# A 31-tap depthwise convolution computed as a product of spectra in a one-core transformer kernel

## The chip, the core and the metric

The kernel runs on one core of a Trainium2 chip. A core has TensorE (matrix products, called PE in the profile, with PEld for its weight loads), VectorE (DVE), ScalarE (ACT), GpSimd (POOL) and SyncE (SP, which here only issues DMAs). The metric is the device time of one execution in microseconds (us), from the chip; lower is better.

## The reference, cut to what matters

Two transformer blocks run one after the other over 256 tokens of width 1024. The change touches the odd layer of the second block alone: its mixer, which runs once, near the end of the program.

```python
def odd_mixer(u, conf_dw, conf_dw_b, conf_ln_g, conf_ln_b, sc_dw):   # u = h @ b_w_in, 256 x 2560
    a, gate, sb, scc, sx = jnp.split(u, [512, 1024, 1536, 2048], axis=-1)
    conf = a * jax.nn.sigmoid(gate)
    conf = depthwise_conv(conf, conf_dw) + conf_dw_b        # 31 taps, 512 channels, over tokens
    conf = jax.nn.silu(group_layer_norm(conf, conf_ln_g, conf_ln_b, 4))   # 4 groups of 128 channels
    sc = sb * depthwise_conv(scc * sx, sc_dw)               # 3 taps
    return jnp.concatenate([conf, sc], axis=-1)

x = x + g1 * (odd_mixer(h @ b_w_in, ...) @ b_w_out)
x = x + g2 * swiglu(modulate(rms_norm(x, norm2_g), sh2, sc2), ffn_w1, ffn_w3, ffn_w2)
```

A depthwise convolution mixes nothing between channels: each output token of a channel is a weighted sum of 31 neighbouring tokens of that channel.

## The kernel before, in words

The function `phase_f` holds the odd layer. It opens its pools, normalises the tokens (`rms_affine`: sums of squares on ACT, a chain of small operations and the scaled rows `xr` on DVE, transposes `aT` on PE, then `ut`, `lhs_hi` on ACT and `lhs_lo` on DVE), runs the products with `b_w_in`, the mixer, the product with `b_w_out` (`residual`) and then the feed-forward part (`ffn(1)`), which ends the program.

Every large product is made from three products of fp32r parts: `split` copies a weight tile `w` to `whi` on ACT (L201), subtracts on DVE or POOL to get `wlo` (L202), and PE multiplies whi by lhs_hi, wlo by lhs_hi and whi by lhs_lo. A tile `w` is 1 MB: it is loaded by an SP DMA into a ring of four (`wtile`), and split in two halves of 128x1024; there are three buffers for halves here. Behind each tile of the layer's weights one tile of another weight, `ada_w`, is loaded and multiplied (`pump`, rate 1), a background job for the feed-forward part. Two forms of product appear in the layer:

- `lin_T`: weights stationary, output with channels on the partitions and 256 tokens along the row (lines L1899 to L1901, 128x256, 48 PE instructions for each 1 MB tile).
- `products`, called by `lin` and `lin_D`: tokens stationary, output with tokens on the partitions and 512 channels along the row (lines L246 to L248, 128x512, 24 PE instructions for each 1 MB tile).

The ten tiles of `b_w_in` go through five calls of `lin_T`: two with half of the gate and half of the value each (`ev_conf`), then `scc`, `sx` and `sb` for the three-tap part. All their halves are split on POOL. `ev_conf` sets the gate on ACT (`osg`), multiplies on DVE into `oconf` with 15 columns of zeros on either side, and then convolves channel block by channel block: 29 of 31 taps are DVE instructions over 128x256 (`conv`: L1947 and then L1945 into `ocv`), and `TAPS` = 2 taps are products with diagonal matrices `odw` on PE (L1968 into `oconv`). After the last `lin_T`, PE adds the transposed `ocv` into `oconv` (L1992). `head_norm` is the group norm (L1485 to L1492, into `oct`), PE transposes `oct` into `oT`, ACT applies silu (L2000, into `osl`), and `split_T` makes the parts for `residual`.

The Tile framework sets the order of each engine's instructions from the order of the code and its readiness; each engine then runs its own queue strictly in order. PSUM has four banks for accumulators (`A`) and four for everything else (`B`).

## Time and profile before

| | |
|---|---|
| time, median of 3 runs | 2397.98 us (2395.06 to 2399.15) |
| time of the profiled execution | 2396.94 us, of which the profile's span is 2395.2 us |
| PE busy over the span | 2199.4 us (92%), 13153 instructions |
| DVE busy | 1287.0 us (54%) |
| ACT, POOL busy | 745.4 us (31%), 459.3 us (19%) |
| bytes read from HBM | 646.58 MB, 270 GB/s over the span |
| mean granted TensorE clock | 0.960 of full |
| place of the odd mixer | about 2035 to 2190 us of the span; `ffn(1)` follows to the end |

Times in rows are counted from the start of the span. A row of a group gives a line, an engine, an operation, its output and inputs by the program's names, and the number of instructions behind an x. One product of fp32 numbers that the code writes appears as two PE instructions in the trace; the fp32r products appear as one.

### The profile page before, as it was taken

The page shows a single profiled execution, that of the slowest core. Times are in us where ns is not written, and L with a number is a line of the kernel's source. Part 1 is how long each engine was busy: PE and PEld are TensorE (multiplying, and loading weights), DVE is VectorE, ACT ScalarE, POOL GpSimd, SP SyncE. Part 2 cuts the span into 40 slices and gives each one's busy share as a digit, 9 for nine tenths or more (in the row PEclk, how much of TensorE's full clock was granted, in tenths as well). Part 3 has the DMA queues.
Part 4 walks back from the last instruction along what each step waited for, and adds up shares of the span by engine and source line. Part 5 has one row for each costly group of instructions (what it writes and reads, how often), then busy time and mean ns, then how long its engine had stood idle before and what let it go on. Part 6 is the DMA issues. An engine that isn't in the chain of part 4 may idle for free.

```text
span 2395.2 us, 35469 instructions
## 1 busy us (share of the span) xinstructions
PE 2199.4 (92%) x13153; PEld 1383.5 (58%) x13154; DVE 1287.0 (54%) x3006; ACT 745.4 (31%) x1263; POOL 459.3 (19%) x424
## 2 busy tenths in 40 slices
PE   7999996899899997999799899997999999868999
PEld 3686774444444442776543333332756997656997
DVE  3354756655466556757833222225764554766554
ACT  2215233211211111444331111111463443414443
POOL 2121300133233335101001211112101000650000
PEclk9999998899999998999899999998999999979999
DMA  8654267799999998443599999999545555737553
GB/s 297 245 203 170 72 214 271 275 377 408 348 408 409 409 409 333 163 176 124 223 356 408 362 408 408 409 409 349 200 148 194 187 184 188 265 117 250 185 179 120
DMA packets 208891, 650.31 MB, mean 272 GB/s; under 512 B 20796, under 2 KB 34093, under 8 KB 197184
## 3 DMA queue, kind: packets, MB, share of 16 engines
q1 hardware_dynamic: 201680, 632.24, 70.4%
q0 software_dynamic: 7024, 15.66, 1.9%
q8 instruction: 107, 1.75, 0.3%
q14 instruction: 80, 0.66, 0.1%
HBM read 646.58 MB, written 1.25 MB: 270 GB/s over the span
## 4 chain that ended last, share of the span: by engine, by line
PE 49%; DMA 13%; DVE 8%; ACT 1%; POOL 1%; issue 1%; SPq 0%; DVEq 0%; ACTq 0%; POOLq 0%
PE gu L842 10%; DMA w<-in_moe_w_up_dram 8%; PE ey L868 5%; PE A L246 4%; PE A L247 4%; PE A L248 4%; PE A L1901 4%; PE A L1900 4%; PE A L1899 4%; DMA w<-in_moe_w_down_dram 4%; DVE ocv L1945 2%; PE ada L314 1%; PE xT L768 1%; PE sc L888 1%; DVE wlo L202 1%
## 5 line engine op out<-in xcount | busy, mean ns | idle before, releaser
L842 PE MATMUL gu<-w,xT 128*32 128x512 f32 (+1 forms) x2880 | 480.9, 603 | 24.3 <-DVEq L996 8.9
L202 DVE TENSOR_TENSOR wlo<-w,whi 128x1024 fp32r<-128x1024 f32 (+3 forms) x240 | 294.4, 1228 | 309.6 <-ACT whi L201 309.3
L201 ACT ACTIVATE whi<-w 128x1024 fp32r<-128x1024 f32 (+3 forms) x264 | 274.1, 1041 | 506.3 <-PE A L248 275.7
L842 PEld LDWEIGHTS gu<-w,xT 128*32 128x32 f32 (+1 forms) x2880 | 139.9, 121 | 310.4 <-issue 245.9
L1901 PE MATMUL A<-lhs_hi,wlo 128*128 128x256 f32 x864 | 246.8, 286 | 13.6 <-POOL wlo L202 13.1
L246 PE MATMUL A<-whi,lhs_hi 128*128 128x512 f32 (+3 forms) x640 | 249.5, 394 | 7.8 <-ACT whi L201 4.4
L247 PE MATMUL A<-wlo,lhs_hi 128*128 128x512 f32 (+3 forms) x640 | 246.2, 385 | 4.4 <-DVE wlo L202 4.2
L1899 PE MATMUL A<-lhs_hi,whi 128*128 128x256 f32 x864 | 247.8, 287 | 0.7 <-ACT whi L201 0.7
L1900 PE MATMUL A<-lhs_lo,whi 128*128 128x256 f32 x864 | 247.2, 286 | 0.0
L248 PE MATMUL A<-whi,lhs_lo 128*128 128x512 f32 (+3 forms) x640 | 244.7, 383 | 0.1
L868 PE MATMUL ey<-w,hT 128*32 128x512 f32 (+1 forms) x1440 | 226.6, 598 | 9.3 <-ACT hT L855 9.2
L892 DVE TENSOR_TENSOR gy<-sc,g 128x512 f32<-128x512 f32 x188 | 121.3, 685 | 209.0 <-PE sc L889 207.1
L893 POOL TENSOR_TENSOR mx<-mx,gy 128x512 f32<-128x512 f32 x124 | 161.1, 1326 | 356.3 <-DVE gy L892 356.2
L1901 PEld LDWEIGHTS A<-lhs_hi,wlo 128*128 128x128 f32 x864 | 167.9, 195 | 14.1 <-POOL wlo L202 13.3
L1899 PEld LDWEIGHTS A<-lhs_hi,whi 128*128 128x128 f32 x864 | 168.2, 195 | 6.8 <-issue 5.0
L1900 PEld LDWEIGHTS A<-lhs_lo,whi 128*128 128x128 f32 x864 | 167.9, 194 | 0.2 <-DVE lhs_lo L256 0.2
L246 PEld LDWEIGHTS A<-whi,lhs_hi 128*128 128x128 f32 x640 | 122.0, 192 | 58.7 <-issue 17.9
L868 PEld LDWEIGHTS ey<-w,hT 128*32 128x32 f32 (+1 forms) x1440 | 68.0, 121 | 148.6 <-issue 121.2
L893 POOL TENSOR_TENSOR xres<-xres,gy 128x512 f32<-128x512 f32 x58 | 74.0, 1289 | 378.7 <-DVE gy L892 377.9
L247 PEld LDWEIGHTS A<-wlo,lhs_hi 128*128 128x128 f32 x640 | 122.5, 191 | 32.9 <-DVE wlo L202 7.3
L248 PEld LDWEIGHTS A<-whi,lhs_lo 128*128 128x128 f32 x640 | 122.3, 191 | 24.9 <-issue 4.0
L882 DVE SCALAR_TENSOR_TENSOR yl<-ey,wsl,yh 128x512 fp32r<-128x512 f32 x62 | 46.4, 750 | 139.2 <-ACT yh L881 137.9
(591 smaller groups left out, 3312.7 us busy)
## 6 DMA issues: line engine op xcount, KB each, us to landing
w<-in_moe_w_gate_dram SPq DMA_DIRECT2D x248, 512.0 KB, 10.2
w<-in_moe_w_up_dram SPq DMA_DIRECT2D x248, 512.0 KB, 10.1
w<-in_moe_w_down_dram SPq DMA_DIRECT2D x248, 512.0 KB, 10.2
w<-in_ada_w_dram SPq DMA_DIRECT2D x88, 1024.0 KB, 6.4
w<-in_ffn_w_dram SPq DMA_DIRECT2D x64, 1024.0 KB, 5.1
w<-in_ab_w_in_dram SPq DMA_DIRECT2D x13, 1024.0 KB, 8.5
w<-in_c_w_qkv_dram SPq DMA_DIRECT2D x12, 1024.0 KB, 5.2
w<-in_ada_w_dram SPq DMA_DIRECT2D x16, 512.0 KB, 10.3
```

What stands on the lines that cost most here:

```text
L201: self.nc.scalar.activation(hv, w, AF.Copy)
L202: (eng or self.nc.vector).tensor_sub(lv, w, hv.bitcast(F32))
L246: nc.tensor.matmul(o, hi[:, kk, ts], wh[:, k], start=at + k == 0, stop=False)
L247: nc.tensor.matmul(o, hi[:, kk, ts], wl[:, k], start=False, stop=False)
L248: nc.tensor.matmul(o, lo[:, kk, ts], wh[:, k], start=False, stop=at + k == nk - 1)
L842: nc.tensor.matmul(pgu[m][a:b], xT[:, j, a:b], w[:, i, k], start=j == 0, stop=j == 7)
L868: nc.tensor.matmul(py[h][a:b], hT[:, j, a:b], w[:, i, k, h * 512:h * 512 + 512], start=j == 0, stop=j == 3)
L892: V.tensor_mul(gy, ps, M.g2[t // 2][:, h * 512:h * 512 + 512])
L893: eng.tensor_add(o, o, gy)
L1899: nc.tensor.matmul(o, wh[:, k, cs], hi[:, kk], start=kk == 0 and c % 2 == 0, stop=False)
L1900: nc.tensor.matmul(o, wh[:, k, cs], lo[:, kk], start=False, stop=False)
L1901: nc.tensor.matmul(o, wl[:, k, cs], hi[:, kk], start=False, stop=kk == 7 and c % 2 == 1)
```

## The change

The 31-tap convolution is computed as a product of spectra. Over 272 samples, which hold 256 tokens and 16 zeros, the convolution wraps around without touching a result. Its 136 frequencies lie at odd halves, so that each has a cosine and a sine part. Three tables of constants are added as inputs: `dft_w` takes the taps to spectra, `dft_t` the tokens, `dft_b` goes back. The steps are:

- At the start of the layer six DMAs on POOL's queue load the two tap tables, the three tables of constants and the bias; three fp32 PE products (`oH`, 31 rows by 512 channels) make the spectra of the taps, and ACT copies them. All of it stands ahead of `rms_affine`.
- Gate and value come from `lin`, with tokens on the partitions and 512 channels along the row, in the place of two calls of `lin_T`.
- A generator `conv_norm` does the rest in three steps, called from `lin_T` behind every tile through `self.between`: behind the first tile of `scc` six fp32 products of 512 columns (`oX`, tokens to spectra) and seven DVE operations (spectra times spectra, into `oY`); behind the second tile of `scc` six fp32 products back (`oconv`, the bias is one more row of the product) and both group norms; behind the second tile of `sx` the eight transposes and silu. Nothing is done at the other calls.
- The first tap of the three-tap convolution moves from DVE to ACT.

The diff, cut to what matters:

```diff
@@ lin_T, behind each tile of weights
+            if self.between:
+                next(self.between)
@@ phase_f
-            self.rms_affine(self.xres, 1, 0, lhs)
             with self.pool("pf") as p:
-                wrow = p.tile([34, 512], F32, name="wrow")
-                nc.gpsimd.dma_start(wrow[:31], I["b_conf_dw_2"][0])
-                nc.gpsimd.dma_start(wrow[31:], I["b_sc_dw_2"][0])
...
-                        nc.scalar.activation(dw[:, c, k], self.ident, AF.Copy, scale=cw[:, c, k:k + 1])
...
+                nc.gpsimd.dma_start(fw, I["dft_w"])
+                nc.gpsimd.dma_start(ft, I["dft_t"])
+                nc.gpsimd.dma_start(fb, I["dft_b"])
+                Y = [p.tile([m, 512], F32, name=f"oY{i}") for i, m in enumerate((128, 128, 33))]
+                nc.gpsimd.dma_start(Y[2][32:], I["b_conf_dw_b_2"])
...
+                    nc.tensor.matmul(ph[:m], fw[:, o:o + m], wrow, start=True, stop=True)
+                    nc.scalar.activation(h, ph[:m], AF.Copy)
...
+                self.rms_affine(self.xres, 1, 0, lhs)
...
-                        V.tensor_mul(conf[:, c, 15:271], ps, sg[:, c])
-                        conv(cv, conf, c, range(TAPS, 31), 0, self.pcol[:, 53 + c:54 + c])
-                        for t in range(2):
-                            for k in range(TAPS):
-                                at = k + t * 128
-                                nc.tensor.matmul(pv[t][:, c * 128:c * 128 + 128], conf[:, c, at:at + 128],
-                                                 dw[:, c, k], start=c == 0 and k == 0, stop=False)
+                def ev_conf(t, ps):
+                    V.tensor_mul(conf[:, t], ps, sg[t])
+                def conv_norm():
+                    px = [self.psB("oX") for _ in parts]
+                    for x, (o, m) in zip(px, parts):
+                        for k in range(2):
+                            nc.tensor.matmul(x[:m], ft[:, k, o:o + m], conf[:, k], start=k == 0, stop=k == 1)
+                    V.tensor_mul(Y[0], px[0], H[0])
+                    V.tensor_mul(q[1], px[0], H[1])
+                    V.tensor_mul(q[0], px[1], H[1])
+                    V.tensor_mul(Y[1], px[1], H[0])
+                    V.tensor_mul(Y[2][:32], px[2][:32], H[2])
+                    V.tensor_sub(Y[0], Y[0], q[0])
+                    V.tensor_add(Y[1], Y[1], q[1])
+                    yield
+                    for t in range(2):
+                        for i, (_, m) in enumerate(((0, 128), (0, 128), (0, 33))):
+                            nc.tensor.matmul(pv, fb[:m, i, t * 128:t * 128 + 128], Y[i], start=i == 0, stop=i == 2)
+                        self.head_norm(pv, ct[t], True, 1e-6)
+                    yield
+                    yield
...
-                for c2 in range(2):
-                    self.lin_T(W, ((512 + 256 * c2, 256), (256 * c2, 256)), lhs, each(ev_conf(c2)), nc.gpsimd)
+                self.early = 8
+                self.lin(W, 8, 512, 512, lhs, (0, 1), ev_gate)
+                self.lin(W, 8, 0, 512, lhs, (0, 1), ev_conf)
+                self.between = conv_norm()
                 self.lin_T(W, ((1536, 512),), lhs, each(ev_scc), nc.gpsimd)
                 self.lin_T(W, ((2048, 512),), lhs, each(ev_sx), nc.gpsimd)
                 self.lin_T(W, ((1024, 512),), lhs, each(ev_sb), nc.gpsimd)
```

Setting `self.early` to 8 keeps the eight halves of gate and value on POOL. What stands on DVE from the multiplication with the gate on is, before (`oconf` the gated value, `ocv` the running sum of the taps, `oscx` the input of the three-tap part):

```order
L1963 TENSOR_TENSOR oconf<-A,osg 128x256 x2
L1947 TENSOR_SCALAR ocv<-oconf,cw,pcol 128x256 x2
L1945 SCALAR_TENSOR_TENSOR ocv<-oconf,cw,ocv 128x256 x56
L1963 TENSOR_TENSOR oconf<-A,osg 128x256 x2
L1947 TENSOR_SCALAR ocv<-oconf,cw,pcol 128x256 x2
L1945 SCALAR_TENSOR_TENSOR ocv<-oconf,cw,ocv 128x256 x56
L318 TENSOR_TENSOR ada_sb<-ada,ada_sb 128x512
L1976 TENSOR_TENSOR oscx<-A,oscc 128x256 x2
```

All 116 instructions of the taps stand between the two halves of the gate and the three-tap part. The same place in the changed kernel (`oX` the spectra of the tokens in PSUM, `oH` those of the taps, `oY` their product, `oq` a helper):

```order
L1968 TENSOR_TENSOR oconf<-A,osg_18671 128x512
L1968 TENSOR_TENSOR oconf<-A,osg_18672 128x512
L1977 TENSOR_TENSOR oY_18516<-oX,oH_18522 128x512
L1978 TENSOR_TENSOR oq<-oX,oH_18526 128x512
L1979 TENSOR_TENSOR oq<-oX,oH_18526 128x512
L1980 TENSOR_TENSOR oY_18517<-oX,oH_18522 128x512
L1982 TENSOR_TENSOR oY_18516<-oY_18516,oq 128x512
L1981 TENSOR_TENSOR oY_18518<-oX,oH_18530 32x512
L1983 TENSOR_TENSOR oY_18517<-oY_18517,oq 128x512
L1497 BN_STATS hn_st<-oconv 128x6 x4
L1499 BN_AGGR hn_mv<-hn_st 128x2 x4
```

Seven operations stand in the place of the taps, and the group norm has moved ahead of the three-tap part, behind which it stood before. On PE, the second visit of the taps on its queue is, before, in the middle of a tile of `scc`:

```order
L1901 MATMUL A<-lhs_hi,wlo 128x256
L1968 MATMUL oconv<-odw,oconf 128x128 x8
L1899 MATMUL A<-lhs_hi,whi 128x256
L1900 MATMUL A<-lhs_lo,whi 128x256
L1901 MATMUL A<-lhs_hi,wlo 128x256
```

Whatever stands behind `oconv` there waits with it for DVE's `oconf`. In the changed kernel the first spectral work on PE's queue is between the two tiles of `scc`:

```order
L1913 MATMUL A<-lhs_hi,wlo 128x256
L1975 MATMUL oX<-oconf,dftT 128x512 x4
L1975 MATMUL oX<-oconf,dftT 32x512 x2
L326 MATMUL ada<-w,cs_1104 32x512 x4
L1911 MATMUL A<-lhs_hi,whi 128x256
```

A whole tile of `scc` (48 instructions) now stands between the last value product and `oX`, and another between `oX` and the way back. On ACT, where the halves of the weights are copied to `whi`, the end of the mixer reads before (the last `whi` of `sb` are among the first row's seven, the next belong to `b_w_out`):

```order
L201 ACTIVATE whi<-w 128x1024 x7
L255 ACTIVATE lhs_hi<-osv 128x256 x3
L201 ACTIVATE whi<-w 128x1024
L255 ACTIVATE lhs_hi<-osv 128x256
L201 ACTIVATE whi<-w 128x1024 x3
L2000 ACT_TABLE_LOAD
L2000 ACTIVATE osl<-oT,pcol 128x256 x2
```

The silu stands there behind weights of `b_w_out`. In the changed kernel:

```order
L213 ACTIVATE whi<-w 128x1024 x3
L2020 ACTIVATE osv<-oscx,cw 128x256 x2
L1999 ACT_TABLE_LOAD
L1999 ACTIVATE osl<-oT,pcol 128x256 x2
L267 ACTIVATE lhs_hi<-osl 128x256 x2
L1999 ACTIVATE osl<-oT,pcol 128x256 x2
L267 ACTIVATE lhs_hi<-osl 128x256 x2
L2020 ACTIVATE osv<-oscx,cw 128x256 x2
L213 ACTIVATE whi<-w 128x1024 x4
```

The silu and the first tap `osv` now stand ahead of the last two halves of `sb`, which are the first two of the last row's four.

## Rows read from the trace of the kernel before

**Rows 1.** Busy time by stretch: us, then PE, PEld, DVE, ACT, POOL, clock, DMA share, GB/s.

```profile
2052.00:2190.00 138.00, 109.90 (x756) 90.97 (x758) 96.93 (x220) 45.62 (x70) 67.74 (x28) 0.89 0.57 210
...
2117.30:2130.50 13.20, 0.23 (x2) 0.03 (x1) 11.67 (x29) 1.03 (x1) 13.20 (x1) 0.62 0.00 0
2155.40:2164.30 8.90, 8.90 (x52) 6.59 (x51) 7.20 (x32) 3.51 (x6) 1.17 (x3) 1.00 1.05 402
2199.50:2395.20 195.70, 190.34 (x1325) 177.72 (x1324) 98.34 (x99) 83.11 (x98) 3.55 (x2) 0.99 0.48 159
```

**Rows 2.** The chain of work that ended last, in order of time, 2062 to 2136 us.

```profile
2062.05 0.12 PE A L1900
...
2067.75 36.42 DVE ocv L1945 x55
...
2105.28 3.78 PE oconv L1968 x16
2109.06 0.21 PE A L1899
...
2113.27 17.32 POOL wlo L202
```

**Rows 3.** Waits from 2030 to 2195 us: who waited for whom, us in total, times, longest.

```profile
PE A L1901 <- POOL wlo L202: 13.1, 1, 13.1
PE oconv L1968 <- DVE oconf L1963: 13.1, 1, 13.1
...
PE aT L153 <- DVE xr L1648: 6.0, 1, 6.0
...
PE oT L153 <- DVE oct L1492: 1.9, 1, 1.9
```

**Rows 4.** PE in order of time: start, us, line, operation, count.

```profile
1807.57 1.88 PE L1874 MATMUL fA<-fourT,fU 128*128 128x512 f32 x4
...
2155.52 1.95 PE L1992 MATMUL oconv<-ident,ocv 128*128 128x128 f32 x16
...
2158.39 0.50 PE L246 MATMUL A<-whi,lhs_hi 128*128 128x512 f32 x1
```

**Rows 5.** DVE and POOL groups of the layer: duration of one, ns min/median/max.

```profile
L1945 DVE SCALAR_TENSOR_TENSOR ocv<-oconf,cw,ocv x112: 467/471/2619, 2067.7 to 2127.9; 128x256 f32<-128x256 f32 x112
...
L202 POOL TENSOR_TENSOR wlo<-w,whi x20: 2339/2407/19214, 2039.6 to 2145.6; 128x1024 fp32r<-128x1024 f32 x20
```

**Rows 6.** DVE in order of time, start first.

```profile
2034.16 0.69 DVE L1663 TENSOR_TENSOR gy<-A,gres 128x512 f32<-128x512 f32 x1 [1.88 <-PE A L248]
...
2039.41 4.86 DVE L1642 TENSOR_SCALAR rA<-adaT 128x16 f32<-128x16 f32 x1
...
2140.21 0.76 DVE L1976 TENSOR_TENSOR oscx<-A,oscc 128x256 f32<-128x256 f32 x2 [11.24 <-PE A L1901]
...
2158.77 0.68 DVE L1485 BATCH_NORM_STATS2 hn_st<-oconv 128x6 f32<-128x128 f32 x3
...
2169.91 1.36 DVE L1492 TENSOR_SCALAR oct<-oconv,hn_mv,hr_y 128x128 f32<-128x128 f32 x4
```

**Rows 7.** POOL in order of time.

```profile
2039.58 4.65 POOL L202 TENSOR_TENSOR wlo<-w,whi 128x1024 fp32r<-128x1024 f32 x2
...
2054.87 0.55 POOL L1917 DMA_DIRECT2D wrow<-in_b_conf_dw_dram  x1 [8.02 <-PE aT L153]
...
2136.84 4.77 POOL L202 TENSOR_TENSOR wlo<-w,whi 128x1024 fp32r<-128x1024 f32 x2 [1.60 <-ACT whi L201]
```

**Rows 8.** ACT in order of time.

```profile
2079.00 1.07 ACT L201 ACTIVATE whi<-w 128x1024 fp32r<-128x1024 f32 x1 [3.01 <-PE A L1900]
...
2174.12 1.28 ACT L2000 ACT_TABLE_LOAD   x1
2175.41 1.02 ACT L2000 ACTIVATE osl<-oT,pcol 128x256 f32<-128x256 f32 x2
2176.32 0.72 ACT L255 ACTIVATE lhs_hi<-osl 128x256 fp32r<-128x256 f32 x2
```

More of the change, by code (lines that the diff above doesn't have):

```diff
@@ L31 @@
 C0, E0, E1, F0, F1 = 4, 4, 4, 1, 4
-TAPS = 2
 NSPL = 3
@@ L1913, in phase_f @@
             lhs = self.lhs_pair(256)
[L1914 removed]
             with self.pool("pf") as p:
[L1916 to L1919 removed]
+                wrow = p.tile([31, 512], F32, name="wrow")
+                nc.gpsimd.dma_start(wrow, I["b_conf_dw_2"][0])
@@ L1920, in phase_f @@
+                cw = p.tile([128, 4, 3], F32, name="cw")
                 pt = self.psB("cw")
                 for c in range(4):
-                    self.tr(pt[:, c * 34:c * 34 + 34], wrow[:, c * 128:c * 128 + 128])
-                V.tensor_copy(cw.rearrange("p c k -> p (c k)"), pt[:, :136])
-                sg = p.tile([128, 4, 256], F32, name="osg")
-                dw = p.tile([128, 4, TAPS, 128], F32, name="odw")
-                for c in range(4):
-                    for k in range(TAPS):
-                        nc.scalar.activation(dw[:, c, k], self.ident, AF.Copy, scale=cw[:, c, k:k + 1])
@@ L1929, in phase_f @@
-                pv = [self.psB("oconv") for _ in range(2)]
-                conf = p.tile([128, 4, 286], F32, name="oconf")
-                V.memset(conf[:, :, :15], 0.0)
-                V.memset(conf[:, :, 271:], 0.0)
+                    self.tr(pt[:, c * 3:c * 3 + 3], wsc[:, c * 128:c * 128 + 128])
+                V.tensor_copy(cw.rearrange("p c k -> p (c k)"), pt[:, :12])
+                self.rms_affine(self.xres, 1, 0, lhs)
+                sg = [p.tile([128, 512], F32, name=f"osg{t}") for t in range(2)]
@@ L1933, in phase_f @@
+                conf = p.tile([128, 2, 512], F32, name="oconf")
                 scx = p.tile([128, 4, 258], F32, name="oscx")
@@ new lines, in ev_conf @@
+                def ev_conf(t, ps):
[5 more added lines that the diff above has]
+                            nc.tensor.matmul(x[:m], ft[:, k, o:o + m], conf[:, k], start=k == 0, stop=k == 1)
+                    q = [self.sb.tile([128, 512], F32, name="oq", tag="s512") for _ in range(2)]
+                    V.tensor_mul(Y[0], px[0], H[0])
[6 more added lines that the diff above has]
+                    yield
+                    ct = []
+                    for t in range(2):
+                        pv = self.psB("oconv")
+                        for i, (_, m) in enumerate(((0, 128), (0, 128), (0, 33))):
+                            nc.tensor.matmul(pv, fb[:m, i, t * 128:t * 128 + 128], Y[i], start=i == 0, stop=i == 2)
+                        ct.append(p.tile([128, 512], F32, name=f"oct{t}"))
+                        self.head_norm(pv, ct[t], True, 1e-6)
+                    yield
+                    yield
+                    for c in range(4):
+                        po = self.psB("oT")
+                        for t in range(2):
+                            self.tr(po[:, t * 128:t * 128 + 128], ct[t][:, c * 128:c * 128 + 128])
+                        u = self.sb.tile([128, 512], F32, name="osl", tag="s512")
+                        nc.scalar.activation(u[:, :256], po[:, :256], AF.Silu, scale=self.pcol[:, 57 + c:58 + c],
+                                             bias=self.pcol[:, 61 + c:62 + c])
+                        self.split_T(mix[0][:, c], mix[1][:, c], u[:, :256])
+                    yield
+                    yield
+                    yield
@@ L1987, in phase_f @@
                 self.lin_T(W, ((1024, 512),), lhs, each(ev_sb), nc.gpsimd)
-                ct = [p.tile([128, 512], F32, name=f"oct{t}") for t in range(2)]
-                for t in range(2):
-                    for c in range(4):
-                        nc.tensor.matmul(pv[t][:, c * 128:c * 128 + 128], cv[:, c, t * 128:t * 128 + 128],
-                                         self.ident, start=False, stop=c == 3)
-                    self.head_norm(pv[t], ct[t], True, 1e-6)
-                for c in range(4):
-                    po = self.psB("oT")
-                    for t in range(2):
-                        self.tr(po[:, t * 128:t * 128 + 128], ct[t][:, c * 128:c * 128 + 128])
-                    u = self.sb.tile([128, 512], F32, name="osl", tag="s512")
-                    nc.scalar.activation(u[:, :256], po[:, :256], AF.Silu, scale=self.pcol[:, 57 + c:58 + c],
-                                         bias=self.pcol[:, 61 + c:62 + c])
-                    self.split_T(mix[0][:, c], mix[1][:, c], u[:, :256])
+                self.between = None
             self.residual(I["b_w_out_2"][0], 8, mix, 1, 0)
@@ L2019, in build @@
         self.first = None
-        self.early = 0
+        self.early, self.between = 0, None
         self.cap = CAPS[0]
```

51 lines of the change are left out of this document (30 added, 21 removed).

## The prediction

> **What bounds the kernel now.** I read the busy time by stretch first. Over the odd mixer, 2052 to 2190 us, PE is busy 109.9 of 138 us, and in 2117.3 to 2130.5 it does nothing while no byte arrives (DMA share 0.00) and its clock is at 0.62 [rows 1]. Then the chain of work: it enters DVE with 55 of the taps for 36.4 us, comes back to PE for `oconv`, and is caught again by one POOL subtraction `wlo` that lasted 17.3 us [rows 2]. The waits say the same from PE's side: 13.1 us for `oconf` (PE's queue holds products of the second gate half, which DVE reaches only after the taps of the first), 13.1 us for `wlo`, 1.9 us for `oct` [rows 3]. The `wlo` was slow because DVE's taps and POOL hold each other off: a tap takes 471 ns as a rule and up to 2.6 us, a `wlo` 2.4 us as a rule and once 19.2 us [rows 5]. So DVE's 31 taps set this stretch, partly through POOL; PE does not. Behind it, in `ffn(1)`, PE is busy 190.3 of 195.7 us at 48% of the DMA engines [rows 1]: what is gained in the mixer is not given back there.
>
> **What goes away on PE.** The waits for `oconf` and for `wlo` have no taps behind them any more, and `oct` is made three tiles of weights earlier: 13.1 + 13.1 + 1.9 = 28.1 us. After each long wait PE ran at the lower of its two clock levels: the 16 `oconv` instructions took 3.78 us [rows 2] and the same 16 at full clock 1.95 [rows 4], and products of 256 columns came every 0.21 us in place of 0.12 [rows 2] for 6 of them after the first wait and 17 after the second, counted in the chain: 2.1 us. Together 3.9 us. The 48 instructions with 128 columns (2 x 16 with `odw`, 16 with `ocv`) go, at 1.9 us for 16 [rows 4]: 5.7 us. Sum: 37.7 us. DVE loses 116 instructions of about 0.4 us, which count only through these waits.
>
> **What comes on PE.** There are fifteen new fp32 products of 512 columns. The nearest row is the Fourier mix of the even layer, also fp32 with 512 columns: four PE instructions, two products as written, in 1.88 us [rows 4], so 0.94 us each. Twelve of them (`oX` there, `oconv` back) stand in the dense stretch: 11.3 us. The three for the taps' spectra (2.8 us) stand ahead of the transposes `aT`, where PE waits 6.0 us for `xr` [rows 3]: I cost them at nothing; without that cover they are 2.8 us, at the lower clock 5.6. Gate and value in 96 products of 512 columns instead of 192 of 256 have as many columns in all, so nothing.
>
> **The start.** POOL's six loads come first on its queue, at 0.55 us [rows 7] 3.3 us. Their memory was the feed-forward part's, so they start with the end of its last product; queued behind them are the stores of `ada`, two `wlo` (4.65 us [rows 7]) and the spectra's products, with `aT` behind these on PE. In the trace those two `wlo` hold up a tiny DVE instruction (`rA`) for 4.86 us [rows 6], and `xr` behind it. Now `xr` stands ahead of `rA` and the `wlo` come later. If `xr` slips through, the start is up to 3 us earlier; if PE is not done with the spectra when `xr` is, up to 3 us later. I take 0.
>
> **The new waits.** First, `oX` to `oconv`: DVE has seven operations on 512 columns at 0.69 us (the row `gy` has this shape and a PSUM input) [rows 6], 4.8 us, and can start on the first spectrum about 1.9 us into `oX`. Two of the seven read SBUF twice as the taps do and may each lose 2.6 us to a `wlo` [rows 5]: finished after 1.9 + 4.8 + 5.2 = 11.9 us. PE reaches `oconv` after six products (5.6) and a tile of weights (48 x 0.12 + 1.0 for `ada` = 6.8): 12.4 us. No wait, at worst 2 us. The other five read one input from PSUM; two such operations took 0.76 us at 2140.2 [rows 6] inside a pair of `wlo` from 2136.8 to 2141.6 [rows 7], so they pass beside POOL. The Trainium skill, page "SBUF — State Buffer", section "Who interferes with whom", has it that a VectorE instruction with at most one SBUF input, outside the two-port modes, does not contend with GpSimd. By it the chain is the 11.9 us above; if all seven could be held, three `wlo` fit and it would be 12.6 us, a wait of 0.2 us. The trace agrees with it.
>
> Second, the norms to `oT`: both ran from 2158.8 to 2171.3 [rows 6], 12.5 us, with other DVE work in between. They now start half-way into the way back and have two tiles of `sx`, 13.6 us, as cover: nothing, at worst 3 us.
>
> Third, ACT: the silu (table load 1.28, four `osl` 2.04, four `lhs_hi` 1.44 [rows 8]) and four `osv` of about 0.5 stand ahead of the last two halves of `sb`; with a `whi` of 1.07 [rows 8] and a `wlo` of 2.4 the next half is ready some 10 us after `oT` begins. PE has the transposes (1 us) and the first tile of `sb` (6.8). I take 2 us, from 0 to 4. Fourth, the 16 `oconv` instructions with `ocv` stood from 2155.52 on, right behind the last product of `sb`, and the first product of `b_w_out` came at 2158.39 [rows 4]; without them the chain from `sb` to its halves on DVE and ACT lies bare: 1.9 us.
>
> **Sum.** 37.7 - 11.3 - 2.0 - 1.9 = 22.5 us off the span of 2395.2: 2372.7. The profiled execution took 2396.94, 1.7 more than its span, and the median is 1.0 above that execution; between the two I forecast 2374 us. With the bounds: no new wait and 3 us at the start make 2367; waits of 2 + 3 + 4 + 1.9 and 3 us later make 2383.
>
> **Rivals.** (1) DVE holds POOL off. One `wlo` of 19.2 us stood through a run of taps [rows 5]. The norms are the longest run now. If POOL waits through all 12.5 us and has two halves of lead (5.7 us), PE waits 6.8 us, and another 1 us goes to the lower clock: 2382. Against it: the norm's operations are short, many read PSUM, and the median of the twenty `wlo` is 2.4 us. The same page of the Trainium skill says that the port pair is held for one instruction by whoever starts first. By that no `wlo` could wait longer than one tap, and this rival would cost nothing; the trace speaks against it with 19.2 us, so I keep it. Chance 0.14.
>
> (2) Slower: the hand-offs lie bare. The three `lin_T` calls have twelve `wlo`; where one meets a DVE operation on the way to `oconv`, `oT` or `sb`, 2.6 us are lost. If each of them struck where PE waits, 31 us, with 1.5 us of lower clock after each of four waits, 6 us: 2374 + 37 = 2411. It decides from nine of the twelve on (9 x 2.6 = 23). For it: the 55 taps of the chain took 36.4 us [rows 2] where 55 x 0.47 = 25.9 would have done [rows 5], over 10 us lost to POOL. Against it: the covers of 12.4 and 13.6 us above, and five of seven products that pass. Chance 0.04.
>
> (3) It does not pay: the weights become the bound. A tile with its `ada` tile is 2.1 MB, 5.2 us at the 402 GB/s of the fullest stretch [rows 1], against 6.8 us on PE; ten and four of them. If load and split, one behind the other in a ring of four, allowed one tile in 8.3 us, 14 x 1.5 = 21 us would be lost: 2395, no difference. Against it: the mean over the mixer is 210 GB/s, half of the fullest stretch [rows 1], and none of the waits above is for a load. Chance 0.06.
>
> (4) More gain: no new wait at all and the earlier start, 2358 to 2366. Chance 0.06.
>
> **How the numbers follow.** The forecast, 2366 to 2381, has the chance 0.70. The range 2364 to 2386 adds (1) and a part of (4). A measurement of this kernel can tell about 0.2% from no change, here 2393.2 and below: faster 0.90 (forecast, (1) and (4)), same 0.06 (rival (3)), slower 0.04 (rival (2)).
>
> **What would show it.** In the profile after: no wait of PE over 4 us between the first value product and the end of `residual`; no `wlo` over 3 us; twelve `oX` and `oconv` products in about 11 us at full clock; the mixer's clock near 1.0 and its DMA rate up to about 250 GB/s; `ffn(1)` as long as before. Waits of PE for `oY` or `oct` speak for (2), a long `wlo` for (1), waits of ACT's `whi` for `w` for (3). The forecast is wrong if the fp32 products cost much over 0.94 us, if the start loses more than 3 us behind POOL's loads, or if what the mixer gains comes back as a wait for weights in `ffn(1)`.

## The result, and the profile after

The changed kernel takes 2372.4 us (median of four runs, 2366.37 to 2373.39); the kernel before, run beside it, 2396.5 (2393.45 to 2399.15). The ratio is 0.9894, with a 95% interval from 0.9874 to 0.9915: faster by 24 us, about 1%, where 22.5 us were forecast (2374). The sum behind the forecast was not as good as its result: the start was off by 3.9 us one way, and the waits that were to come and the end of the stretch together by 7.5 the other way.

The profiled execution after took 2366.37 us, the fastest of the four. In it `ffn(0)`, which the change doesn't touch, ends 5.0 us earlier than in the execution profiled before (2030.52 against 2035.53). That is no part of the change (in the runs below that leave everything ahead of it alone, it ends anywhere from 2030.5 to 2037.4), so I measure both from there: from the end of `ffn(0)`'s last product to the end of the last `b_w_out` product. This **stretch** takes 154.3 us before and 128.4 after. Stretches of the trace after, with columns as in [rows 1]: the start, the mixer from its first product to the last of `b_w_out`, and `ffn(1)`:

```profile
2030.50:2050.90 20.40, 15.32 (x57) 5.03 (x57) 12.45 (x34) 8.41 (x18) 10.68 (x13) 0.67 0.63 225
2050.90:2159.00 108.10, 107.50 (x633) 78.12 (x634) 41.47 (x99) 43.39 (x62) 49.77 (x26) 1.00 0.77 276
2168.70:2364.60 195.90, 190.34 (x1325) 177.76 (x1323) 98.22 (x99) 83.01 (x97) 3.56 (x2) 0.99 0.49 159
```

In the mixer PE is now busy 107.5 of 108.1 us at full clock, where it was 109.9 of 138 at 0.89 [rows 1]. DVE fell from 96.9 to 41.5 us, and `ffn(1)` takes as long as before. All waits of PE from 2030 to 2160 us (who waited for whom, total, times, longest):

```profile
PE oH L1946 <- DMA dftW<-in_dft_w_dram: 5.1, 1, 5.1
PE A L1913 <- POOL wlo L214: 0.6, 2, 0.4
```

The waits of [rows 3] for `wlo`, `oconf` and `oct` are gone but for 0.6 us, and so is the wait for `xr`, in whose place one for `dftW` stands. The new products on PE, and the low halves on POOL from 2050 us on (count, ns min/median/max, first and last start):

```profile
L1975 PE MATMUL oX<-oconf,dftT x12: 592/592/617, 2084.1 to 2089.0; 128*128 128x512 f32 x8, 128*32 128x512 f32 x4
L1989 PE MATMUL oconv<-oY,dftB x12: 589/592/697, 2096.2 to 2101.5; 128*128 128x512 f32 x8, 33*128 33x512 f32 x4
L214 POOL TENSOR_TENSOR wlo<-w,whi x18: 2342/2394/3384, 2055.6 to 2125.9; 128x1024 fp32r<-128x1024 f32 x18
```

Six products are twelve PE instructions. `oX` lasts from 2084.13 to 2089.56, `oconv` from 2096.20 to 2102.10: 11.3 us together. The longest `wlo` is 3.4 us, where [rows 5] had 19.2. PE's way to the first mixer product (start, us, line, count, idle before):

```profile
2030.45 1.92 PE L326 MATMUL ada<-w,cs 128*32 128x512 f32 x16
2037.45 5.59 PE L1946 MATMUL oH<-wrow,dftW 31*128 31x512 f32 x6 [5.08 <-DMA dftW<-in_dft_w_dram]
2042.97 0.58 PE L165 MATMUL cw<-ident,wsc 3*128 3x3 f32 x4
2043.48 1.11 PE L165 MATMUL ada<-ident,ada_sb 128*128 128x128 f32 x4
2044.53 1.94 PE L326 MATMUL ada<-w,cs 128*32 128x512 f32 x8
2046.40 1.54 PE L165 MATMUL aT<-ident,xr 128*128 128x128 f32 x6
...
2050.90 0.50 PE L258 MATMUL A<-whi,lhs_hi 128*128 128x512 f32 x1
```

Here the change lost something. PE's queue holds `oH`, then `ada`'s transposes and products, then `aT`. All of them wait for the small table `dftW`, then `oH` takes 5.6 us at the lower clock, and only then comes work that before was done ahead of `xr`. POOL issued that load as its third, and DVE still waits behind the two `wlo` on POOL, now with `rs_a` in place of `rA` [rows 6]:

```profile
2031.91 0.53 POOL L1936 DMA_DIRECT2D dftW<-in_dft_w_dram  x1
...
2035.22 4.65 POOL L214 TENSOR_TENSOR wlo<-w,whi 128x1024 fp32r<-128x1024 f32 x2
```

```profile
2034.73 5.24 DVE L193 SCALAR_TENSOR_TENSOR rs_a<-rs_a 128x1 f32<-128x1 f32 x2
```

The stretch, piece by piece, in us after `ffn(0)`'s last product:

| | before | after | gain |
|---|---|---|---|
| first mixer product | 16.50 | 20.38 | -3.9 |
| from there to the end of `sb`'s last product | 103.65 | 81.37 | 22.3 |
| from there to the first `b_w_out` product | 2.71 | 0.93 | 1.8 |
| the `b_w_out` products | 31.40 | 25.71 | 5.7 |
| sum | 154.27 | 128.39 | 25.9 |

### The profile page after: what moved, and what is told of

It reads as the page before. It is cut to its first block, busy times and chain, and to the rows that moved or that the text cites. A ratio compares the mean times of both kernels' runs of the same rounds, so it can differ in the third digit from the quotient of the medians.

```text
span 2364.6 us, 35118 instructions
## 1 busy us (share of the span) xinstructions
PE 2199.8 (93%) x13039; PEld 1371.0 (58%) x13040; DVE 1233.5 (52%) x2889; ACT 746.3 (32%) x1260; POOL 443.6 (19%) x428
## 4 chain that ended last, share of the span: by engine, by line
PE 50%; DMA 12%; DVE 6%; issue 2%; ACT 2%; POOL 1%; DVEq 0%; ACTq 0%; POOLq 0%; SPq 0%
PE gu L854 10%; DMA w<-in_moe_w_up_dram 8%; PE ey L880 5%; PE A L258 5%; PE A L259 5%; PE A L260 4%; PE A L1913 4%; PE A L1911 4%; PE A L1912 4%; DMA w<-in_moe_w_down_dram 4%; PE xT L780 1%; PE ada L326 1%; PE sc L900 1%; DVE wlo L214 1%; PE sc L901 1%
## 5 line engine op out<-in xcount | busy, mean ns | idle before, releaser
L854 PE MATMUL gu<-w,xT 128*32 128x512 f32 (+1 forms) x2880 | 480.6, 601 | 22.8 <-DVEq L1008 8.8
L258 PE MATMUL A<-whi,lhs_hi 128*128 128x512 f32 (+3 forms) x672 | 261.6, 393 | 7.9 <-ACT whi L213 4.4
L259 PE MATMUL A<-wlo,lhs_hi 128*128 128x512 f32 (+3 forms) x672 | 258.4, 385 | 4.9 <-DVE wlo L214 4.8
L260 PE MATMUL A<-whi,lhs_lo 128*128 128x512 f32 (+3 forms) x672 | 256.9, 383 | 0.1
L1911 PE MATMUL A<-lhs_hi,whi 128*128 128x256 f32 x800 | 228.2, 286 | 1.0 <-ACT whi L213 1.0
L1913 PE MATMUL A<-lhs_hi,wlo 128*128 128x256 f32 x800 | 227.1, 284 | 1.1 <-POOL wlo L214 0.6
L1912 PE MATMUL A<-lhs_lo,whi 128*128 128x256 f32 x800 | 227.7, 285 | 0.0
L1911 PEld LDWEIGHTS A<-lhs_hi,whi 128*128 128x128 f32 x800 | 154.3, 193 | 6.3 <-issue 3.4
L1913 PEld LDWEIGHTS A<-lhs_hi,wlo 128*128 128x128 f32 x800 | 154.1, 193 | 1.7 <-POOL wlo L214 1.0
L1912 PEld LDWEIGHTS A<-lhs_lo,whi 128*128 128x128 f32 x800 | 154.4, 193 | 0.2 <-DVE lhs_lo L268 0.2
L259 PEld LDWEIGHTS A<-wlo,lhs_hi 128*128 128x128 f32 x672 | 128.3, 191 | 33.9 <-DVE wlo L214 9.0
```

Of the source, the lines that this page charges most:

```text
L258: nc.tensor.matmul(o, hi[:, kk, ts], wh[:, k], start=at + k == 0, stop=False)
L259: nc.tensor.matmul(o, hi[:, kk, ts], wl[:, k], start=False, stop=False)
L260: nc.tensor.matmul(o, lo[:, kk, ts], wh[:, k], start=False, stop=at + k == nk - 1)
L854: nc.tensor.matmul(pgu[m][a:b], xT[:, j, a:b], w[:, i, k], start=j == 0, stop=j == 7)
L1911: nc.tensor.matmul(o, wh[:, k, cs], hi[:, kk], start=kk == 0 and c % 2 == 0, stop=False)
L1912: nc.tensor.matmul(o, wh[:, k, cs], lo[:, kk], start=False, stop=False)
```

## The experiments

The theory has three parts: (a) DVE's taps caused both long waits, the second through POOL; (b) with the taps gone PE bounds the mixer, and the spectra cost what their products cost there; (c) the start costs something, because of `dftW` and `oH`. In the table, the time is a median of four runs where the text gives a ratio, else one run; the kernel before took 2393.9 to 2397.0 beside them. "Start" is the first mixer product, after `ffn(0)`'s last one.

| kernel | time, us | start | stretch |
|---|---|---|---|
| before | 2396.5 | 16.5 | 154.3 |
| changed | 2372.4 | 20.4 | 128.4 |
| one tap on DVE (from before) | 2359.8 | 15.8 | 121.2 |
| ten taps on PE (from before) | 2392.0 | 15.8 | 152.1 |
| no spectra | 2358.1 | 16.5 | 113.9 |
| `oX`, `oconv` twice | 2376.9 | 20.3 | 139.3 |
| hand-offs bare | 2375.5 | 20.4 | 132.7 |
| idle: separate operations, SBUF | 2376.4 | 20.7 | 136.2 |
| idle: separate operations, PSUM | 2375.3 | 19.9 | 130.6 |
| idle: taps in place | 2385.4 | 20.6 | 143.2 |
| `oH` behind the gate | 2371.0 | 15.8 | 128.4 |
| taps loaded early | 2369.6 | 15.3 | 124.1 |
| low halves on DVE | 2369.7 | 20.5 | 128.5 |
| both at the start | 2365.5 | 13.5 | 123.5 |

### (a) The taps: one, and twenty-one

```diff
-                        conv(cv, conf, c, range(TAPS, 31), 0, self.pcol[:, 53 + c:54 + c])
+                        conv(cv, conf, c, range(TAPS, TAPS + 1), 0, self.pcol[:, 53 + c:54 + c])
```

> The kernel before with one of the 29 taps that DVE had for each chunk of channels; the other 28 are left out of the computation. Measured from the end of ffn(0)'s last product to the end of the last b_w_out product, the kernel before takes 154.3 us, the changed one 128.4. Theory (DVE's taps are the cause of both waits of 13.1 us, the second one through POOL): both waits go and the lower clock behind them, no wlo lasts over 3.5 us, and the stretch takes 126 us (123 to 130). Rival (the first wait is the order of the second gate's and value's halves on PE and ACT, the second one POOL's own): a wait of 8 us or more stays and the stretch takes 140 us or more.

All waits of PE in the stretch, and the low halves:

```profile
PE aT L153 <- DVE rs_y L182: 5.9, 1, 5.9
PE ada L153 <- DVE ada_sb L318: 0.8, 1, 0.8
```

```profile
L202 POOL TENSOR_TENSOR wlo<-w,whi x20: 2341/2398/2471, 2036.7 to 2114.4; 128x1024 fp32r<-128x1024 f32 x20
```

Both long waits went, the one for `oct` with them, and no `wlo` lasts over 2.5 us. The stretch lost 33.1 us. That is more than the 28.3 expected here (121.2 lies below the range of 123 to 130), and close to what the prediction itself has for waits and clock, 28.1 + 3.9 = 32.0. Part (a) holds as a cause. The size was then varied:

```diff
-TAPS = 2
+TAPS = 10
```

> The kernel before with 10 taps as products with a diagonal on PE in place of 2, so that DVE has 21 for each chunk of channels in place of 29; the same result. Theory (the length of the two waits follows the number of taps on DVE, at 0.47 to 0.66 us each): 32 taps less on DVE, 15 to 21 us; the two waits shrink from 26.2 us to 6 to 12, PE gets 64 products of 128 columns at 0.12 us, 7.6 us, and ACT 32 more diagonals at the start: 154.3 - 17 + 7.6 = 145 us (140 to 151) from the end of ffn(0)'s last product to the end of the last b_w_out product. Rival (a wait is not a matter of the number of taps but of one wlo caught by any run of them): a wait for wlo of 10 us or more stays, 152 us or more.

```profile
PE A L1901 <- POOL wlo L202: 5.9, 3, 4.6
PE ada L314 <- DMA w<-in_ada_w_dram: 3.3, 1, 3.3
PE oconv L1968 <- DVE oconf L1963: 1.4, 1, 1.4
```

```profile
L202 POOL TENSOR_TENSOR wlo<-w,whi x20: 2333/2384/9384, 2036.5 to 2145.2; 128x1024 fp32r<-128x1024 f32 x20
L1968 PE MATMUL oconv<-odw,oconf x160: 275/275/583, 2069.2 to 2109.1; 128*128 128x128 f32 x160
```

The stretch came out where the rival had it, 152.1, but not for the rival's reason. The waits for `wlo` and `oconf` did shrink, from 26.2 to 7.3 us, although two `wlo` were still caught by a run of taps, for 9.4 and 6.4 us. My price for PE was wrong: 64 more fp32 products are 128 more PE instructions (160 against 32 before), at the 0.12 us of [rows 4] 15.6 us and not 7.6, and a wait of 3.3 us for a weight tile is new. So a tap moved to PE with a diagonal costs 0.49 us there for each chunk of channels, more than the 0.40 us that DVE is relieved of.

### (b) The price of the spectra

```diff
-                        for k in range(2):
+                        for k in (0, 1, 0, 1):
...
-                        for i, (_, m) in enumerate(((0, 128), (0, 128), (0, 33))):
+                        for i, m in ((0, 128), (1, 128), (2, 33)) * 2:
```

> The changed kernel with each of the twelve products oX and oconv done twice, the same result. Theory (PE is the bound of the whole stretch, these products have nothing to hide behind, and cost 0.94 us each): 128.4 + 11.3 = 139.7 us (138.5 to 141.5) from the end of ffn(0)'s last product to the end of the last b_w_out product. Rival (they stand in time in which PE would wait for halves or weights): less than 6 us more, under 134.4.

Measured 139.3, that is 10.9 us for twelve more products: 0.91 each, with nothing to hide behind. Then the whole of it left out:

```diff
-                    ph = self.psB("oH")
-                    nc.tensor.matmul(ph[:m], fw[:, o:o + m], wrow, start=True, stop=True)
...
-                            nc.tensor.matmul(x[:m], ft[:, k, o:o + m], conf[:, k], start=k == 0, stop=k == 1)
...
-                        pv = self.psB("oconv")
+                        pv = conf[:, t]
```

> The changed kernel without the spectra: no oH, oX, products of spectra on DVE and oconv; the norms read gate times value as it is, so the convolution is left out of the computation. Theory (the price of the spectra is 11.3 us of dense products and some 5 us at the start, where dftW's load and oH stand ahead of the transposes aT): 128.4 - 11.3 - 5 = 112 us (110 to 115) from the end of ffn(0)'s last product to the end of the last b_w_out product, the first product at about 15.5 us in place of 20.4. Rival (the start is set by xr, which is held behind POOL's low halves, so oH costs nothing there): first product at 19 to 20 us, 117 us in all.

Start 16.5, stretch 113.9, within the theory's range. The price of the spectra is 14.5 us: 3.9 at the start, and 10.6 in the mixer.

The prediction's covers for the hand-offs were tested by making them bare:

```diff
-                self.between = conv_norm()
...
-                self.between = None
+                for _ in conv_norm():
+                    pass
```

> The changed kernel with the way there, the norms and the way back not stepped through the three lin_T calls but all of it behind the last of them. Theory (the products in between cover DVE's seven operations and the norms): PE waits 3 to 5 us for oY, 7 to 9 us for oct, and 2 to 4 us are lost to the lower clock; b_w_out starts with the half of its rows that needs no silu, so that the silu stays covered. 128.4 + 15 = 143 us (139 to 149) from the end of ffn(0)'s last product to the end of the last b_w_out product. Rival (DVE is so much relieved that the hand-offs cost little by themselves, and the gain is only that of the taps): 133 us or less.

PE behind the last `sb` product (the `b_w_out` products left out):

```profile
2124.58 5.00 PE L1975 MATMUL oX<-oconf,dftT 128*128 128x512 f32 x11
...
2135.54 7.65 PE L1989 MATMUL oconv<-oY,dftB 128*128 128x512 f32 x12 [3.08 <-DVE oY L1982]
...
2144.85 0.27 PE L165 MATMUL oT<-ident,oct 128*128 128x128 f32 x1
```

The stretch grew by 4.3 us only, not by 15; the rival's number was right. The wait for `oY` came as expected, 3.1 us, with `oconv` at 7.65 us partly at the lower clock in place of 5.9. The wait for `oct` did not come: the Tile framework put products of `b_w_out` between `oconv` and the first `oT`, and more between the `oT`. So stepping the work through the three `lin_T` calls by hand is worth 4 us of the 26. The other 22 come without it.

### How DVE holds POOL off

The prediction kept a rival for a `wlo` that waits through a run of DVE operations, on the strength of one row of 19.2 us [rows 5]. Three idle runs on DVE, whose results nobody reads, show what such a run needs. The first and the second differ in where one input lies:

```diff
+                    idle = p.tile([128, 512], F32, name="oidle")
+                    for _ in range(30):
+                        V.scalar_tensor_tensor(idle[:, :256], conf[:, 0, :256], cw[:, 0, 0:1], sg[0][:, :256],
+                                               op0=OP.mult, op1=OP.add)
```

> The changed kernel with 30 idle operations on DVE behind the seven products of the spectra: scalar_tensor_tensor on 256 columns with both inputs in SBUF, as the taps of the kernel before had them, into a tile that nobody reads. Theory (a run of DVE operations with two SBUF inputs holds a POOL instruction off for as long as the run lasts): the idle run takes 12 to 20 us, one wlo lasts over 8 us, PE waits 3 us or more for it. Rival (the hold lasts for one instruction at a time, POOL and DVE take turns): no wlo over 4 us, and single idle operations of 2.5 us among them instead.

> The same 30 idle operations on DVE with one input in PSUM (the first spectrum) and one in SBUF. Theory (operations that read PSUM pass beside POOL, as five of the seven products of the spectra did): no wlo over 3 us, no idle operation over 1 us, no wait of PE for wlo over 1 us; the stretch is at most 3 us longer, for the norms start later. Rival (any dense run on DVE holds POOL off, whatever it reads): one wlo over 8 us as with both inputs in SBUF.

With both inputs in SBUF (DVE, then POOL, then the idle group):

```profile
2084.61 12.26 DVE L1986 SCALAR_TENSOR_TENSOR oidle<-oconf,cw,osg 128x256 f32<-128x256 f32 x16
```

```profile
2085.37 2.49 POOL L214 TENSOR_TENSOR wlo<-w,whi 128x1024 fp32r<-128x1024 f32 x1 [1.56 <-ACT whi L213]
2088.23 2.63 POOL L214 TENSOR_TENSOR wlo<-w,whi 128x1024 fp32r<-128x1024 f32 x1 [0.38 <-ACT whi L213]
```

```profile
L1986 DVE SCALAR_TENSOR_TENSOR oidle<-oconf,cw,osg x30: 467/485/2677, 2079.7 to 2109.5; 128x256 f32<-128x256 f32 x30
```

The theory fell here. Both `wlo` began inside the run and passed at once. It was DVE that waited: for each of them one idle operation lasted 2.5 us in place of 0.485. The stretch grew by 7.8 us, mostly since the framework placed 16 idle operations ahead of `oY` (PE waited 4.1 us for it, and its granted clock was 0.61 in the 4 us behind). With one input in PSUM no operation waited, and the stretch grew by 2.2 us:

```profile
L1986 DVE SCALAR_TENSOR_TENSOR oidle<-oX,cw,osg x30: 448/470/485, 2093.3 to 2113.0; 128x256 f32<-128x256 f32 x30
```

It agrees with the Trainium skill, page "SBUF — State Buffer", section "Who interferes with whom", by which a VectorE instruction with at most one SBUF input, outside the two-port modes, doesn't contend with GpSimd. But what then had held POOL for 19 us? The idle operations began 0.52 us apart and lasted 0.485, a gap of 0.04 us each. The taps of the kernel before lasted 0.47, and each began before the one ahead of it had ended, 22.25 us for 56 of them and so one in 0.397 us (DVE of the kernel before):

```profile
2106.12 22.25 DVE L1945 SCALAR_TENSOR_TENSOR ocv<-oconf,cw,ocv 128x256 f32<-128x256 f32 x56
```

So the third run had the taps' own form, two chains in turn:

```diff
+                    for k in range(31):
+                        for h in (idle[:, :256], idle[:, 256:]):
+                            x, w = Y[0][:, k:k + 256], cw[:, 0, 0:1]
...
+                                V.scalar_tensor_tensor(h, x, w, h, op0=OP.mult, op1=OP.add)
```

> The changed kernel with 60 idle operations on DVE behind the products of the spectra in the very form of the taps of the kernel before: two chains in turn, each adding into its own tile in place, both inputs in SBUF. In the idle run with a tile that was overwritten, one operation began 0.04 us after the end of the one before and POOL always came in between; the taps of the kernel before began every 0.396 us and lasted 0.47, without such a gap. Theory (POOL is held off for as long as DVE's operations overlap): operations every 0.40 us, about 24 us for the run, and at least one wlo of over 5 us with a wait of PE for it. Rival (they take turns also without a gap, and the 19.2 us of the kernel before had another cause): no wlo over 4 us, and one idle operation of 2.5 us for every wlo. In both cases the norms start late and PE waits 5 to 10 us for oct.

The run on DVE, the low halves on POOL (as a group, and the three from 2099.24 on in one row), and PE's longest wait:

```profile
2095.97 23.82 DVE L1991 SCALAR_TENSOR_TENSOR oidle<-oY,cw,oidle 128x256 f32<-128x256 f32 x60
```

```profile
L214 POOL TENSOR_TENSOR wlo<-w,whi x20: 2342/2389/22755, 2039.6 to 2137.2; 128x1024 fp32r<-128x1024 f32 x20
```

```profile
2099.24 27.43 POOL L214 TENSOR_TENSOR wlo<-w,whi 128x1024 fp32r<-128x1024 f32 x3 [6.86 <-ACT whi L213]
```

```profile
PE A L1913 <- POOL wlo L214: 11.0, 1, 11.0
```

A `wlo` that began at 2099.24, inside the run, ended at 2122.00, 2.2 us after it: 22.8 us, and PE waited 11.0 for it. (The norms were late too, but PE, held by `wlo`, waited only 0.7 us for `oct`.) That rebuilds the second wait of the kernel before in the changed one. The same page of the Trainium skill, section "SBUF: two separate sides", says that the pair of ports is held for one instruction by whoever starts first. In the idle run with gaps the trace agrees; here it does not, as one POOL instruction waited through some 50 of DVE's.

The missing gap alone doesn't decide it, though. In the kernel before, taps overlap in both runs. Of the `wlo` that began inside them, seven in the first run got in within some 0.3 us, each making one tap last 2.6, and only one, in the second run, was held. Two rows of POOL show one of the seven, and the held one, which took 19.2 us, with the two behind it:

```profile
2080.15 2.60 POOL L202 TENSOR_TENSOR wlo<-w,whi 128x1024 fp32r<-128x1024 f32 x1 [1.53 <-ACT whi L201]
...
2111.36 23.88 POOL L202 TENSOR_TENSOR wlo<-w,whi 128x1024 fp32r<-128x1024 f32 x3 [19.03 <-ACT whi L201]
```

The traces show one difference. Those that got in, the two of the idle run with gaps among them, came at most 2.2 us after the start of the run or after the last tap that had been held. The four that were held (22.8, 19.2, and 9.4 and 6.4 with ten taps on PE) came after 3.3 us or more of undisturbed operations, and all four ended 2.2 to 2.3 us behind the run. So the gap of 0.04 us and the time since the last interruption were not told apart, and whether either decides stays open.

### (c) The start

```diff
-                H = []
-                for i, (o, m) in enumerate(parts):
-                    ph = self.psB("oH")
...
                 self.lin(W, 8, 512, 512, lhs, (0, 1), ev_gate)
+                H = []
+                for i, (o, m) in enumerate(parts):
+                    ph = self.psB("oH")
```

> The changed kernel with the three oH products and their copies moved behind the products of the gate. Theory (dftW's load and oH at the lower clock, ahead of aT in PE's queue, cost the start 4 to 5 us): aT begins at about 10 us after ffn(0)'s last product in place of 15.9, the first mixer product at 15.5 to 17 in place of 20.4; oH costs 2.8 us at full clock where it now is. 128.4 - 4.3 + 2.8 = 127 us (125.5 to 128.5) to the end of the last b_w_out product. Rival (the start is set by something else, as xr behind POOL's loads or the halves of the first weights): the first product stays at 19.5 us or later, 131 us in all.

The first product came at 15.8 us as expected, but the stretch stayed at 128.4, the upper end of what was expected (2371.0 us; ratio to before 0.9901, 0.9884 to 0.9917). PE around the moved products:

```profile
2063.79 0.39 PE L260 MATMUL A<-whi,lhs_lo 128*128 128x512 f32 x1
2064.11 2.99 PE L2026 MATMUL oH<-wrow,dftW 31*128 31x512 f32 x6
2067.03 1.94 PE L326 MATMUL ada<-w,cs 128*32 128x512 f32 x8
2068.90 0.80 PE L258 MATMUL A<-whi,lhs_hi 128*128 128x512 f32 x1
...
2070.33 0.39 PE L258 MATMUL A<-whi,lhs_hi 128*128 128x512 f32 x1
```

The stretch behind `oH`, with columns as in [rows 1]:

```profile
2067.10:2070.30 3.20, 3.20 (x12) 1.30 (x12) 0.00 (x0) 0.66 (x2) 2.14 (x1) 0.50 1.02 332
```

`oH` cost 3.0 us here, and behind it, without any wait, PE fell to its lower clock for 3.2 us: eight `ada` instructions took 1.94 us, as they do at the lower clock, where 1.06 is usual. So 4.6 us were won at the start, and 3.0 and 1.6 given back.

```diff
+            q = self.top.enter_context(self.pool("taps"))
+            self.wrow = q.tile([31, 512], F32, name="wrow")
+            nc.gpsimd.dma_start(self.wrow, I["b_conf_dw_2"][0])
+            self.fw = q.tile([31, 288], F32, name="dftW")
+            nc.gpsimd.dma_start(self.fw, I["dft_w"])
             self.ffn(0)
```

> The changed kernel with the taps and the table dftW in memory of their own, loaded ahead of ffn(0). Theory (PE waits for dftW's transfer, which cannot start before ffn(0)'s memory is free): oH runs at once at the lower clock, 5.6 us, inside the wait for xr, aT begins at about 10 us, the first mixer product comes at 15.5 to 17 us in place of 20.4, and the stretch from ffn(0)'s last product to the last b_w_out product takes 124 us (122.5 to 125.5) in place of 128.4. Rival (the start is set by xr or by POOL's queue): 127.5 us or more.

Start 15.3, stretch 124.1: close to the theory's numbers. But the framework did more than I asked for. With its inputs there, `oH` moved to the beginning of `ffn(0)`:

```profile
1847.44 2.95 PE L1948 MATMUL oH<-wrow,dftW 31*128 31x512 f32 x6
```

There it takes 3.0 us at full clock, outside the stretch, so of 4.3 us 1.3 remain. The time is too coarse for that: 2369.6 us, ratio 0.9897 (0.9880 to 0.9913) where the changed kernel has 0.9894. The kernel shows what the start costs, not that `oH` hides in the wait for `xr`. With `oH` gone from there, the next wait of PE is for a weight tile of `ada`:

```profile
2044.03 1.92 PE L326 MATMUL ada<-w,cs 128*32 128x512 f32 x2 [3.44 <-DMA w<-in_ada_w_dram]
```

```diff
-                eng = nc.gpsimd if self.early > 0 else None
+                eng = nc.gpsimd if 0 < self.early <= 8 else None
...
-                self.early = 8
+                self.early = 11
...
+                self.early = 0
                 self.between = conv_norm()
```

> The changed kernel with the first three low halves wlo of the mixer on DVE, behind the normalisation in its order, in place of POOL. Theory (a small DVE instruction of the normalisation waits 5 us behind POOL's two wlo, but aT waits for oH as well, which ends 12.5 us after ffn(0)'s last product): xr is ready at about 5 us in place of 9.7, aT begins at about 13 in place of 15.9, and one low half of 1.1 us then lies bare: 128.4 - 2.9 + 1.1 = 126.6 us (125 to 128.5) to the end of the last b_w_out product. Rival (xr is what sets the start): first product 5 us earlier, 123.5 us or less; rival (low halves on DVE hold up the transposes' own halves): 129 or more.

> The changed kernel with both edits of the start: the taps and dftW loaded ahead of ffn(0), and the first three low halves on DVE. Theory (the start has two chains, dftW and oH on PE's side, POOL's wlo and xr on DVE's; both must go): oH until about 6 us, aT begins at 6 to 7 us after ffn(0)'s last product, the first mixer product at 12 to 14 us in place of 20.4: 121 us (119.5 to 123) in place of 128.4, so about 2365 us where the changed kernel has 2372.4. Rival (with the low halves on DVE the start gains nothing over the early load alone): 124 us or more.

Alone, this edit changed nothing in the stretch (start 20.5, 128.5, the theory's upper end; 2369.7 us, ratio 0.9894, 0.9878 to 0.9911): `aT` began at 16.1 us, not at 13, still behind `oH`, `cw` and `ada`. In the changed kernel PE's side sets the start, not `xr`. Both edits together gave the earliest first product, 13.5 us, but a stretch of 123.5 us, just above the range I had given (121, up to 123). `oX` began only 0.6 us earlier than with the early load alone, for the first products ran at the lower clock (0.50 and 0.78 in two stretches of 4 us from 2050.9 on):

```profile
2050.90:2054.90 4.00, 3.35 (x11) 2.65 (x12) 2.73 (x5) 3.67 (x11) 0.00 (x0) 0.50 0.98 372
2054.90:2058.90 4.00, 4.00 (x17) 3.13 (x16) 1.52 (x4) 3.35 (x8) 0.00 (x0) 0.78 0.42 170
```

It has the lowest median of those that leave nothing out, 2365.5 us (2364.4 to 2368.9; ratio 0.9876, 0.9860 to 0.9893). By the trace it is worth 128.4 - 123.5 - 3.0 = 1.9 us against the changed kernel. The two intervals overlap, so that it beats the changed kernel is likely, not shown.

## Why the prediction came out right, and where it did not

**What goes away: right.** 28.1 us of waits and 3.9 of lower clock were forecast, 32.0 in all. With the taps cut the stretch lost 33.1 us, and after the change none of these waits is left. The reading that [rows 1] to [rows 5] gave, DVE's taps and through them POOL, is confirmed by removal (one tap) and by rebuilding (idle taps in place). Why this `wlo` was held and seven others were not, the reading doesn't say, and neither do the runs.

**What comes on PE: right.** 11.3 us for twelve products at 0.94; the trace has 11.3, doubling gives 10.9. From the first mixer product to the end of `sb` the working makes waits 26.2 + clock 3.9 + 32 products of 128 columns 3.9 - 11.3 = 22.7 us, and the gain there is 22.3. Two terms of about 1 us that the working has at nothing offset each other inside it: gate and value are faster in the new form (a product of 512 columns every 0.23 us, two of 256 took 0.24), and the eight `oT` transposes have moved in.

**The start: wrong.** It was taken at 0, within 3 us; it cost 3.9. The step that failed is the sentence that costs the three products for the taps' spectra at nothing, since PE waits 6.0 us for `xr` there [rows 3]. A wait covers only work that is ready. `oH` waited 5.1 us itself, as `dftW` landed 5.4 us after its issue, and then ran at the lower clock for 5.6 us, a price that the text names. What it did not count is what stood behind `oH` in PE's queue: `ada`'s transposes and products, which before had been done ahead of `xr`. Without the spectra the start is 16.5 us, as before. The way that the text saw for an earlier start didn't open either: `xr` did not slip through, DVE was held for 5.2 us on `rs_a` ahead of it. A start that loses more than 3 us is one of the signs that the prediction itself gives for being wrong.

**The new waits: too dear.** 3.9 us were taken: 2.0 for ACT, 1.9 for the chain from `sb` to `b_w_out`. Neither came. The pause ahead of `b_w_out` fell from 2.71 to 0.93 us, about what the 16 `oconv` instructions had taken (1.95), and all waits for `wlo` come to 0.6 us. From `oX` to `oconv` and from the norms to `oT` nothing was lost, as forecast; DVE's seven operations ran from 2086.05 to 2090.88 without being held up, and PE reached `oconv` at 2096.20. Part of that is luck: no `wlo` ran beside the two that read SBUF twice. The worst case given there, 12.6 us with three `wlo`, leaves out the 1.9 us before the first spectrum; with them it is 14.5, a wait of 2.1.

**The end: left out.** The `b_w_out` products gained 5.7 us, where the sum has only the wait of 1.9 for `oct`. The clock falls behind that wait too, to 0.59 (the kernel before, with columns as in [rows 1]):

```profile
2168.40:2172.40 4.00, 4.00 (x12) 3.09 (x13) 2.70 (x10) 0.00 (x0) 0.00 (x0) 0.59 1.06 421
```

Products of `b_w_out` came 0.43 us apart there in place of 0.23, an estimated 1.9 us in all. And the eight `oT` transposes, by an estimate some 1.9 us with what they hold up, now stand in the mixer. (With one tap, where `oT` stands there without a wait for `oct`, these products took 27.9 us: 3.5 less than before for the wait and the clock, 2.2 more than after for `oT`.) The working counted the lower clock behind the two long waits, and not behind the short one.

So the start is off by -3.9 us, the mixer by -0.4, the new waits and the end together by +7.5 (the sum has 1.95 + 1.9 - 2.0 - 1.9 there, the table 1.8 + 5.7): 22.5 + 3.2 = 25.7, where the stretch has 25.9. The medians have 24.1. The forecast of 2374 us is good partly because the errors offset each other. It also stands 1.5 us below the 2375.5 that its sum gives when it is taken off the median of 2397.98; and counted from 2374 the later of its two bounds is 2384, not 2383.

**The rivals.** (1) DVE holds POOL off: the mechanism exists, and at 22.8 us it can be larger than I priced it. The runs have it only in long runs without gaps that read SBUF alone (one without gaps that reads PSUM was not tried). The norms are short operations, many of them on PSUM, and the longest `wlo` of the mixer is 3.4 us. That is over the 3 us given as a sign, but PE waited 0.4 us at most. (2) Bare hand-offs: no `wlo` struck on the way as this rival had it, and the hand-offs made bare cost 4.3 us, not 37. (3) Weights: PE waits for no weight tile in the mixer, at 276 GB/s where 250 were forecast. (4) More gain: no new waits, as it said, but a later start.

## What to carry to other kernels

Ask of an operation that is to hide in a wait whether its own inputs are there by then, and what stands behind it in that engine's queue: here a table of 35 KB, loaded when its memory came free, moved a whole queue back by 4 us. A convolution along the tokens with 31 taps is cheaper as a product of spectra (14.5 us) than as taps on DVE (33.1 us for 28 of the 29), whose dense runs hold up POOL as well, or as diagonals on PE (0.49 us for a tap and chunk, so an estimated 60 us for 124). Before you arrange hand-offs by hand, see what the framework puts there by itself: here the arrangement by hand was worth 4 us.

## What was new about the hardware

- One POOL instruction took 22.8 us in place of 2.4, held through a run of overlapping DVE operations with both inputs in SBUF (19.2 in the kernel before). With gaps of 0.04 us between them POOL entered at once, and one DVE operation took 2.5 us in its turn. Seven POOL instructions entered a run without gaps as well, none of them later than 2.2 us after its start or its last interruption.
- The granted clock fell to 0.50 for 3.2 us without any wait of PE, behind six fp32 instructions of 31 rows, some 17 us after it had risen. The same six at 1847 us, near the beginning of `ffn(0)`, were followed by products at full pace (0.12 us apart). What makes the difference stays open.
- fp32 products go as two PE instructions: 0.91 to 0.94 us for 512 columns at full clock, 1.86 for those of the spectra at the lower one.
